# The first gate group of mixer B in seven block products, and pairs of heads 28 slots apart, in a hybrid convolution and attention layer

## The chip, the cores and the metric

The kernel runs on one core of one Trainium2 chip. The metric is the device time of one execution in microseconds; of several runs the median is taken. A lower time is better.

## What is computed

One decoder layer on 512 tokens of width 2048, in float32, with two mixers side by side:

```
h = rms_norm(x, norm_g)
a_val, a_glu, a_gate, q, k, v, b_gate = split(h @ w_in)     # seven blocks of 1024 columns

u = a_val * sigmoid(a_glu)                                  # mixer A
u = causal_depthwise_conv(u, conv_w, conv_b)                # 31 taps
u = silu(layer_norm(u, conv_norm_g, conv_norm_b))
y_a = (u @ conv_pw_w + conv_pw_b) * silu(a_gate)

q, k = rms_norm per head (16 heads of 64)                   # mixer B
o = dilated_attention_mixture(q, k, v)                      # (128,1), (512,4), (2048,16)
y_b = o * silu(b_gate)

out = x + concat(y_a, y_b) @ w_out
```

The three dilated patterns share one softmax: a table adds the logarithm of the number of patterns that see a key to its score, or a large negative number.

## The kernel before

**Precision.** All large products take float32 operands as two float16 halves: a high part and the low remainder. A product is three matmuls (high times high, high times low, low times high; `tri`, lines 414 to 416). The high halves are copies on ScalarE (ACT), the low halves scalar_tensor_tensor on VectorE (DVE, all through the wrapper at line 82). Scales that keep the halves in range come from sums of squares ("bounds": `measure` and `row_squares`, an ACT pass into `junk`, line 192).

**Groups and units.** The input product is cut into groups of 512 output columns, listed in `GROUPS` in the order in which TensorE (PE) takes them: `vg` 0 to 3 (value and GLU gate of mixer A), `q`, `k`, `v` and `bg` (gate of B) of each half of the heads, `ag` (gate of A); then `pw` 0 and 1 (the pointwise projection, which reads the split convolution result `u16`), `wb` and `wa` (output product). A group of the input product has four units of 512 rows of weights; `pw` has two. A unit of a plain group has eight slots of six 512-column matmuls each. `vg` 0 and 1 are computed in float32.

**Seven block products.** Groups in `SEVEN` take a two-by-two block scheme with seven products instead of eight (`input_products`). Sums of weight blocks are made by accumulating DMAs on POOL's queue and by two DVE subtractions; sums of activation blocks (`tx`) are made once. Each half of a block sum is split by itself (`hi` on ACT, `lo` on DVE, five and four slots ahead of its matmuls), the products land in four PSUM banks, and ACT copies (`copy`) and DVE joins (`joint`, `fourth`) put them together before `out` hands a quarter on. Such a group has 28 slots of twelve 256-column matmuls; the slot clock counts them as 32.

**Slots, calendar and planner.** All instructions are put out in an order written by hand. A clock counts slots, eight to a unit (unit 32 begins at slot 256, `pw` 0 at slot 448). `after(n, fn)` puts work n slots later. In every slot, what is due goes first, then `run_conv`, then the slot's matmuls. Each engine works its own instructions strictly in that order, so a wait holds up all that stands behind it on its engine.

**The convolution** is a generator (`conv`). Its 240 taps are DVE instructions on 512 columns, two channel blocks at a time. `run_conv` gives it DVE time: the wrapper charges every DVE instruction with `START` (180 ns) and 25/24 ns per element, each slot takes `PACE` off (1480 once pairs run), and taps go in while the balance is negative. A `yield n` in the generator waits n slots. After the last tap comes the layer norm: mean (matmul L576), differences and squares, variance (`token_rsqrt`, matmul L395), the row of reciprocal roots (matmul L408, copy L409), then per channel block a multiplication, a Silu (L609) and the split into `u16` (L316 and a DVE low half). Mean and variance are held back while a pair of heads is in its first eight slots:

```python
while any(0 <= clock[0] - n < 8 for n in at_pair.values()):
    yield 1
```

At the start of a unit of `pw`, splits that it needs and that are not yet put out are forced.

**Attention** works on pairs of heads (`two_heads`): scores (L741) on PE in slots 0 and 3 of a pair, the softmax's maxima on DVE, exponentials on ACT (L754), high and low halves of the probabilities (L765, `low`), a DMA transpose on SP's queue (`turn`), and the products with v (L782) at the pair's end, in the slot in which the next pair starts. `attention` puts eight pairs at every 32nd slot: 226, 258, 290, 322, 354, 386, 418, 450. The score buffers (`att` pool) hold the sums `tx` until the last group in seven products is done.

**Gates.** A gate group's results go through Silu into `slot` tiles; `gate_o` multiplies a pair's output with its gate and adds its squares to the bound of the output product. `b0_parts` splits the first half of B's output and is put out 10 slots ahead of `pw`.

**Buffers.** Raw weights have a ring of 8, split weights (`part`) 4 tiles, `slot` 35, `tmp` 4, `att` 4; PSUM has 4 banks for products and 4 for the rest. The split of unit i + 1 (`wh`, L301) is put out in the first slot of unit i and takes the tiles of unit i - 1.

Of the kernel before, what the change touches and what calls it, by code (L numbers as in the profile page):

```python
# [15 lines left out]
AF = mybir.ActivationFunctionType  # L16
# [16 lines left out]
H = S // 2  # L33
WARM = 9
KU = 4
PERIOD = {0: 32, 1: 32}
PHASE = 2
START = 180
NORM_FROM = 37
PACE = 1230  # L40
RMS_EPS = 1e-6
# [6 lines left out]

GROUPS = [("vg", 0), ("vg", 1), ("vg", 2), ("vg", 3), ("q", 0), ("k", 0), ("v", 0), ("bg", 0), ("q", 1), ("k", 1), ("v", 1),
          ("ag", 0), ("ag", 1), ("bg", 1), ("pw", 0), ("pw", 1)]  # L50
JOINED = (0, 1)
GROUPS += [("wb", g) for g in range(4) if g not in JOINED] + [("wa", g) for g in range(4)]
OUT_K = {"wb": (2,), "wa": (3, 0, 1)}

SEVEN = (("vg", 3), ("q", 0), ("v", 0))
LAST_SEVEN = SEVEN[-1]
# [30 lines left out]
def layer(ctx: ExitStack, tc: tile.TileContext, xt, w1, w2, w3, g_in, conv_w, conv_b,  # L87
# [34 lines left out]
    def after(n, fn):  # L122

        calendar.setdefault(clock[0] + max(n, 1), []).append(fn)
# [384 lines left out]
    def evac_qk(half_i, t, ps, is_k):  # L509
        r = evac_scale(("k" if is_k else "q", half_i))  # L510
        z = slot("z")
        sq = temp("sq")
        if is_k:
            V.scalar_tensor_tensor(by_head(z), by_head(ps), r, gp[:, None, :].to_broadcast([P, 8, DH]),
                                   op0=OP.mult, op1=OP.mult)
        else:
            A.activation(z, ps, AF.Copy, scale=r)
        A.activation(sq, ps, AF.Square, scale=r)
        n = [2, 6 + 4 * t, 7 + 4 * t, 9 + 4 * t]
        if is_k and ("v", half_i) in SEVEN:  # L520
# [24 lines left out]
    def conv():  # L545
# [24 lines left out]
        for i in (6, 7):  # L570
            V.tensor_add(acc, acc, cv[i])
        yield 3
        while any(0 <= clock[0] - n < 8 for n in at_pair.values()):
# [10 lines left out]
        for i in range(8):  # L584
            V.tensor_sub(cv[i], cv[i], mean_sb)
            if len(squares) > 1:
                V.tensor_add(acc2, acc2, squares.pop(0))
            if i == 0:
                A.activation(acc2, cv[i], AF.Square)
            else:  # L590
                squares.append(temp("lnsq"))
                A.activation(squares[-1], cv[i], AF.Square)
# [12 lines left out]
        for i in range(8 + 2):  # L605
            if i < 8:
                V.tensor_mul(cv[i], cv[i], row)
            if 1 <= i < 8 + 1:
                A.activation(cv[i - 1], cv[i - 1], AF.Silu, scale=lng[:, i - 1:i], bias=lnb[:, i - 1:i])  # L609
# [81 lines left out]
    def b0_parts():  # L691
        y = yf["b0"]
        s = scales["yb0"][0]
        for k in range(4):
            after(2 * k, lambda k=k: plain("b0", k, s))
        for k in range(2):
            after(6 + 3 * k, lambda k=k: y_sums("d", y, k, k + 2))
            for n, name in enumerate(("t34d", "t12d")):
                after(9 + 3 * k + n, lambda name=name, k=k: block(name, k, s))

# [16 lines left out]
    def two_heads(pair):  # L717
# [77 lines left out]
        plan = [(0, lambda: scores(((3,),))), (3, lambda: scores(((0, 2), (1,))))]  # L795
        for a, e in ((0, 7), (1, 11)):
            h = (13, 18)[a]
            plan += [(6, lambda a=a: shift(a)), (e + 4, lambda a=a: roots(a)), (h + 6, lambda a=a: turn(a))]
            for i in range(NT):
                plan += [(e, lambda a=a, i=i: exps(a, i))]  # L800
                plan += [(h + i // 2, lambda a=a, i=i: high(a, i)), (h + 3 + i // 2, lambda a=a, i=i: low(a, i))]
        return plan, values, put
# [8 lines left out]
    def attention(hf):  # L811
        start = max(clock[0] + 28, max(at_pair.values(), default=0) + PERIOD[0])
        start += (PHASE - start) % 8
        for p4 in range(4):
            at_pair[4 * hf + p4] = start + p4 * PERIOD[hf]

            def begin(pair=4 * hf + p4):
# [8 lines left out]
                after(PERIOD[hf] - (pair == 7), lambda: end_pair(pair))  # L826
            after(at_pair[4 * hf + p4] - clock[0], begin)
# [326 lines left out]
    def input_products(i0):  # L1154
# [82 lines left out]
        def out(name):  # L1237
# [6 lines left out]
            if kind == "vg":  # L1244
# [10 lines left out]

                after(1, mul)
            elif kind == "v":
                if n == 0:
# [5 lines left out]
            else:  # L1264
# [9 lines left out]

                norm_qk(group, t, sq, (2, 5, 6, 8), to)

# [72 lines left out]

    calendar.setdefault(8 * of_group["pw", 0][0] - 10, []).append(b0_parts)  # L1350
    for i in range(n_plain):
# [137 lines left out]
```

## Time and profile before

| | |
|---|---|
| median of 3 runs | 813.09 us (812.22 to 813.32) |
| profiled execution, time | 812.95 us |
| its span, first to last instruction | 811.2 us |
| granted TensorE clock | 1.000 |
| busy: PE, DVE, ACT, POOL | 805.5, 707.2, 561.3, 136.2 us |

The span lies within the execution's time; the 1.75 us between them are outside the instructions. In rows of instructions the first number is the start in microseconds from the span's start, the second the duration, then engine, line, operation, output and inputs; in square brackets is the engine's idle time just before, and what ended it. Matmul rows overlap: a 512-column matmul shows 0.38 us while the next one starts after 0.216.

### The profile page before, as it was taken

The numbers are of one execution on the slowest core, as the hardware profiler recorded it, in microseconds if no ns is written. First come the engines' busy times: TensorE is split into PE (matmuls) and PEld (weight loads), VectorE is DVE, ScalarE is ACT, GpSimd is POOL, SyncE is SP. The second block draws the span as 40 slices with busy tenths as digits, with TensorE's granted clock in tenths as the row PEclk, the third lists the DMA queues.
The fourth block names the chain that finished last, engine by engine and source line by source line (L and its number), as shares of the span: only waits on it lengthen the run. The fifth ranks groups of instructions, "written<-read, shape, count | busy, mean of one in ns | idle before, by whom it ended". The sixth has DMA issues, their size and how long they took to land.

```text
span 811.2 us, 13603 instructions
## 1 busy us (share of the span) xinstructions
PE 805.5 (99%) x5341; PEld 508.8 (63%) x5341; DVE 707.2 (87%) x1188; ACT 561.3 (69%) x788; POOL 136.2 (17%) x147
## 2 busy tenths in 40 slices
PE   9999999999999999999999999999999999999998
PEld 6888745888646854444444444444444447888887
DVE  6668999878989979999999989996689799979885
ACT  6667687577756688586756747587699968965541
POOL 0001021322223400004012010000100003432420
PEclk9999999999999999999999999999999999999999
DMA  9952345983875882526573634426352397898752
GB/s 337 355 212 91 117 93 144 136 255 57 308 150 108 121 296 94 128 104 169 143 182 102 164 112 125 118 88 165 104 120 102 110 278 165 170 249 198 131 103 68
DMA packets 100000, 127.19 MB, mean 157 GB/s; under 512 B 62560, under 2 KB 85344, under 8 KB 90720
## 3 DMA queue, kind: packets, MB, share of 16 engines
q1 hardware_dynamic: 80544, 107.37, 42.2%
q0 software_dynamic: 19104, 18.88, 16.3%
q8 instruction: 41, 0.67, 0.3%
q14 instruction: 23, 0.19, 0.1%
q10 hardware_dynamic: 288, 0.07, 0.0%
HBM read 88.56 MB, written 4.19 MB: 114 GB/s over the span
## 4 chain that ended last, share of the span: by engine, by line
PE 92%; DVE 4%; ACT 2%; DMA 1%; issue 1%; POOL 0%; ACTq 0%; DVEq 0%
PE ps_l L414 24%; PE ps_l L415 24%; PE ps_l L416 24%; PE ps_l L895 10%; PE ps_s L415 2%; PE ps_s L414 2%; PE ps_s L416 2%; PE ps_o L782 2%; PE ps_s L741 2%; DVE ws L82 1%; DMA pt<-hl 1%; DVE wl L82 1%; ACT junk L192 0%; DMA wf<-w_dram 0%; DVE cv L82 0%
## 5 line engine op out<-in xcount | busy, mean ns | idle before, releaser
L82 DVE SCALAR_TENSOR_TENSOR cv<-u,cw,cv 128x511 f32<-128x511 f32 (+14 forms) x240 | 162.0, 728 | 0.4 <-ACT cv L552 0.4
L192 ACT ACTIVATE junk<-wf 128x2048 uint8<-128x2048 f32 x68 | 129.2, 1900 | 9.4 <-DMA wf<-w_dram 9.0
L414 PE MATMUL ps_l<-x,wh 128*128 128x512 f16 x320 | 121.3, 379 | 0.4 <-DVE glu L82 0.4
L416 PE MATMUL ps_l<-x,wl 128*128 128x512 f16 x320 | 121.3, 379 | 0.0
L415 PE MATMUL ps_l<-x,wh 128*128 128x512 f16 x320 | 121.3, 379 | 0.0
L301 ACT ACTIVATE wh<-wf,ws 128x2048 f16<-128x2048 f32 x42 | 83.7, 1994 | 52.0 <-PE ps_l L415 50.2
L82 DVE SCALAR_TENSOR_TENSOR wl<-wf,ws,wh 128x2048 f16<-128x2048 f32 x43 | 100.9, 2346 | 12.1 <-ACT wh L301 12.1
L414 PE MATMUL ps_l<-wh,x 128*128 128x512 f16 x256 | 97.1, 379 | 0.0
L416 PE MATMUL ps_l<-wh,x 128*128 128x512 f16 x256 | 97.0, 379 | 0.0
L415 PE MATMUL ps_l<-wl,x 128*128 128x512 f16 x256 | 97.0, 379 | 0.0
L82 DVE SCALAR_TENSOR_TENSOR ws<-wf,ws 128x1024 f16<-128x1024 f32 x70 | 89.2, 1279 | 7.0 <-ACT ws L1173 4.5
L414 PEld LDWEIGHTS <-wh 128*128 128x128 f16 x448 | 43.9, 98 | 51.5 <-issue 4.0
L416 PEld LDWEIGHTS <-wl 128*128 128x128 f16 x448 | 43.8, 98 | 50.0 <-DVE wl L82 0.4
L415 PEld LDWEIGHTS <-wh 128*128 128x128 f16 x448 | 43.8, 98 | 47.1 <-issue 0.8
L895 PE MATMUL ps_l<-xr,wr 128*128 128x512 f32 x288 | 69.9, 398 | 0.1
L895 PEld LDWEIGHTS ps_l<-xr,wr 128*128 128x128 f32 x288 | 54.5, 190 | 13.7 <-ACT xr L339 1.0
L206 POOL TENSOR_SCALAR ws<-ws 128x1 f32<-128x1 f32 x20 | 9.4, 470 | 306.9 <-DVE ws L82 259.8
L414 PEld LDWEIGHTS <-x 128*128 128x128 f16 x352 | 34.4, 98 | 32.5 <-issue 1.9
L416 PEld LDWEIGHTS <-x 128*128 128x128 f16 x352 | 34.4, 98 | 31.3
L415 PEld LDWEIGHTS <-x 128*128 128x128 f16 x352 | 34.4, 98 | 30.1
L1173 ACT ACTIVATE ws<-wf,ws 128x1024 f16<-128x1024 f32 x42 | 47.1, 1138 | 5.7 <-PE ps_l L416 4.8
L170 POOL TENSOR_TENSOR ss<-ss,half 128x8 f32<-128x8 f32 x16 | 31.5, 1970 | 116.4 <-DVE ss L82 116.3
(265 smaller groups left out, 1871.3 us busy)
## 6 DMA issues: line engine op xcount, KB each, us to landing
wf<-w_dram SPq DMA_DIRECT2D x72, 1024.0 KB, 5.2
wf<-wf POOLq DMA_DIRECT2D x30, 512.0 KB, 6.3
x<-xt_dram SPq DMA_DIRECT2D x16, 256.0 KB, 6.6
res<-xt_dram SPq DMA_DIRECT2D x8, 512.0 KB, 6.7
out_dram<-res SPq DMA_DIRECT2D x15, 256.0 KB, 3.8
wf<-w_dram SPq DMA_DIRECT2D x7, 512.0 KB, 7.2
wf<-wf POOLq DMA_DIRECT2D x12, 256.0 KB, 5.8
wf<-w_dram SPq DMA_DIRECT2D x2, 256.0 KB, 3.4
```

The costliest lines, as they stand in the source:

```text
L82: return getattr(self.engine, name)(out, src, *args, **kw)
L170: G.tensor_tensor(ap, ap, half.to_broadcast(list(ap.shape)), op=OP.pow)
L192: A.activation(junk[:, :n], src, AF.Square, scale=scale, accum_out=acc)
L206: G.tensor_scalar(scale, scale, 1e-30, 2.0 ** (-2 * top), op0=OP.max, op1=OP.mult)
L301: A.activation(parts[i][0], raw[i], AF.Copy, scale=wscale[units[i][3:]][0])
L414: T.matmul(ps, ah, bh, start=first, stop=False, skip_group_check=more)
L415: T.matmul(ps, ah, bl, start=False, stop=False, skip_group_check=more)
L416: T.matmul(ps, al, bh, start=False, stop=last, skip_group_check=more)
L741: T.matmul(ps[i, a], qk["q", hf][p4 // 2][rows, p4 % 2, q, i * P:w], qk["k", hf][p4 // 2][rows, p4 % 2, k, :w], start=n == 0, stop=n == 2)
L782: T.matmul(po[rows, i * P:(i + 1) * P], vs[hf][j // 2][:, j % 2, 2 * p4 + a, vp * DH:(vp + 1) * DH], got["t", a][:, pp * (ALL // P) + FROM ...
L895: T.matmul(banks[group, m], wt[:, a, m * P:(m + 1) * P], xk[b], start=k == 0 and a == b == 0, stop=k == KC - 1 and a == 1)
L1173: A.activation(t[:, 0], block(name, pair), AF.Copy, scale=wscale[group][0])
```

## The change

- `bg` 0 goes in front of `v` 0 and into `SEVEN`. The order is now q, k, bg, v (slots 128 to 255). Its quarters go through Silu in `out`, eight halves of 256 columns; two tiles come together as one gate, and `gate_o` is called.
- `bg` 1 goes in front of `ag` 1: `bg` 1 has slots 384 to 415, `ag` 1 has 416 to 447.
- Pairs of heads stand every 28 slots, from slot 258 (60 slots behind the end of `k` 0): 258, 286, 314, 342, 370, 398, 426, 454. The steps within a pair are drawn together: exponentials at 7 and 10, high halves from 11 and 15, low halves two slots behind them, transposes at 16 and 20. The products of the last pair stay at slot 481.
- `PACE` goes from 1230 to 1300. The yields in the layer norm are shorter.
- `b0_parts` is put out 1 slot ahead of `pw` and in closer steps.
- Normalisation of q and k in `input_products` is put out two to four slots later; the copy `p5` of `bg` and `v` takes a `tmp` tile instead of a `slot` tile.

```diff
-PERIOD = {0: 32, 1: 32}
+PERIOD = 28
...
-PACE = 1230
+PACE = 1300
...
-GROUPS = [("vg", 0), ("vg", 1), ("vg", 2), ("vg", 3), ("q", 0), ("k", 0), ("v", 0), ("bg", 0), ("q", 1), ("k", 1), ("v", 1),
-          ("ag", 0), ("ag", 1), ("bg", 1), ("pw", 0), ("pw", 1)]
+GROUPS = [("vg", 0), ("vg", 1), ("vg", 2), ("vg", 3), ("q", 0), ("k", 0), ("bg", 0), ("v", 0), ("q", 1), ("k", 1), ("v", 1),
+          ("ag", 0), ("bg", 1), ("ag", 1), ("pw", 0), ("pw", 1)]
...
-SEVEN = (("vg", 3), ("q", 0), ("v", 0))
+SEVEN = (("vg", 3), ("q", 0), ("bg", 0), ("v", 0))
...
-        if is_k and ("v", half_i) in SEVEN:
+        if is_k and half_i == 0:
...
@@ conv
-        yield 3
+        yield 2
...
-            yield 1 + i % 2
+            yield 1
...
-        yield 4
+        yield 3
...
-            yield 1
+            yield (i + 1) % 2
             if i >= 2:
                 u16[i - 2] = split16(cv.pop(i - 2), scales["u"][0], "u16")
...
@@ b0_parts
-            after(2 * k, lambda k=k: plain("b0", k, s))
+            after(1 + k, lambda k=k: plain("b0", k, s))
...
-            after(6 + 3 * k, lambda k=k: y_sums("d", y, k, k + 2))
+            after(4 + 3 * k, lambda k=k: y_sums("d", y, k, k + 2))
...
@@ two_heads
-        for a, e in ((0, 7), (1, 11)):
-            h = (13, 18)[a]
-            plan += [(6, lambda a=a: shift(a)), (e + 4, lambda a=a: roots(a)), (h + 6, lambda a=a: turn(a))]
+        for a, e in ((0, 7), (1, 10)):
+            h = (11, 15)[a]
+            plan += [(6, lambda a=a: shift(a)), (e + 3, lambda a=a: roots(a)), (h + 5, lambda a=a: turn(a))]
...
@@ attention
-        start = max(clock[0] + 28, max(at_pair.values(), default=0) + PERIOD[0])
+        start = max(clock[0] + (28 if hf else 60), max(at_pair.values(), default=0) + PERIOD)
...
@@ input_products
-            got[to] = slot("cb")
+            got[to] = temp("cb") if to == "p5" and kind in ("bg", "v") else slot("cb")
...
+            elif kind == "bg":
+                for m in range(2):
+                    i = 4 * g + 2 * x + m
+                    if ("bg", i) not in u_part:
+                        u_part["bg", i] = slot("gate")
+                    A.activation(u_part["bg", i][:, z * H:(z + 1) * H], pair[:, m], AF.Silu)
+                    halves["bg", i] = halves.get(("bg", i), 0) + 1
+                    if halves["bg", i] == 2:
+                        bg[i] = u_part.pop(("bg", i))
+                        after(1, lambda i=i: gate_o(i))
...
-                norm_qk(group, t, sq, (2, 5, 6, 8), to)
+                norm_qk(group, t, sq, (2, 7, 8, 10) if n == 0 else (4, 9, 10, 12), to)
...
-    calendar.setdefault(8 * of_group["pw", 0][0] - 10, []).append(b0_parts)
+    calendar.setdefault(8 * of_group["pw", 0][0] - 1, []).append(b0_parts)
```

More of the change, by code (lines that the diff above doesn't have):

```diff
@@ L694, in b0_parts @@
         for k in range(4):
-            after(2 * k, lambda k=k: plain("b0", k, s))
+            after(1 + k, lambda k=k: plain("b0", k, s))
         for k in range(2):
-            after(6 + 3 * k, lambda k=k: y_sums("d", y, k, k + 2))
+            after(4 + 3 * k, lambda k=k: y_sums("d", y, k, k + 2))
             for n, name in enumerate(("t34d", "t12d")):
-                after(9 + 3 * k + n, lambda name=name, k=k: block(name, k, s))
+                after(6 + 3 * k + n, lambda name=name, k=k: block(name, k, s))
     def y_parts(s, v):
@@ L795, in two_heads @@
         plan = [(0, lambda: scores(((3,),))), (3, lambda: scores(((0, 2), (1,))))]
-        for a, e in ((0, 7), (1, 11)):
-            h = (13, 18)[a]
-            plan += [(6, lambda a=a: shift(a)), (e + 4, lambda a=a: roots(a)), (h + 6, lambda a=a: turn(a))]
+        for a, e in ((0, 7), (1, 10)):
+            h = (11, 15)[a]
+            plan += [(6, lambda a=a: shift(a)), (e + 3, lambda a=a: roots(a)), (h + 5, lambda a=a: turn(a))]
             for i in range(NT):
                 plan += [(e, lambda a=a, i=i: exps(a, i))]
-                plan += [(h + i // 2, lambda a=a, i=i: high(a, i)), (h + 3 + i // 2, lambda a=a, i=i: low(a, i))]
+                plan += [(h + i // 2, lambda a=a, i=i: high(a, i)), (h + 2 + i // 2, lambda a=a, i=i: low(a, i))]
         return plan, values, put
@@ L811, in attention @@
     def attention(hf):
-        start = max(clock[0] + 28, max(at_pair.values(), default=0) + PERIOD[0])
+        start = max(clock[0] + (28 if hf else 60), max(at_pair.values(), default=0) + PERIOD)
         start += (PHASE - start) % 8
         for p4 in range(4):
-            at_pair[4 * hf + p4] = start + p4 * PERIOD[hf]
+            at_pair[4 * hf + p4] = start + p4 * PERIOD
             def begin(pair=4 * hf + p4):
@@ L825, in begin @@
                         after(n, fn)
-                after(PERIOD[hf] - (pair == 7), lambda: end_pair(pair))
+                after(PERIOD - (pair == 7), lambda: end_pair(pair))
             after(at_pair[4 * hf + p4] - clock[0], begin)
```

## The prediction

> **What bounds the kernel now.** I began with the busy table and the chain of waits, then asked what PE waited for, then cut the span into stages.
>
> ```profile
> span 811.2 us, 13603 instructions
> PE 805.5 (99%) x5341; PEld 508.8 (63%) x5341; DVE 707.2 (87%) x1188; ACT 561.3 (69%) x788; POOL 136.2 (17%) x147
> ...
> PE 92%; DVE 4%; ACT 2%; DMA 1%; issue 1%; POOL 0%; ACTq 0%; DVEq 0%
> ...
> PE ps_l L414 <- DVE glu L82: 0.4, 1, 0.4
> ...
> PE ps_l L415 <- DVE ws L82: 0.2, 1, 0.2
> PE ps_o L782 <- DMA pt<-hl: 0.2, 1, 0.2
> PE ps_s L741 <- DVE gate L82: 0.2, 1, 0.2
> ```
>
> The last rows are three of the five waits that PE had after its start; the five, from 0.4 down to 0.2, are 1.3 us together. So the time is the number of matmuls times their pitch, and a change pays on PE or nowhere, unless it opens a wait. DVE is at 87%, which is no bound on the average, but it has deadlines.
>
> ```profile
> 212.58 0.38 PE L414 MATMUL ps_l<-wh,x 128*128 128x512 f16 x1
> ...
> 254.04 0.27 PE L414 MATMUL ps_l<-ws,x 128*128 128x256 f16 x1
> ...
> 290.75 0.38 PE L414 MATMUL ps_l<-x,wh 128*128 128x512 f16 x1
> ...
> 175.50:212.60 37.10, 36.88 (x340) 32.90 (x338) 31.91 (x40) 26.35 (x31) 9.33 (x8) 1.00 0.66 155
> 254.00:290.75 36.75, 36.75 (x338) 32.90 (x337) 33.34 (x43) 22.83 (x28) 14.60 (x11) 1.00 0.86 148
> ```
>
> The first three rows are the first matmuls of three groups in a row. k of the first half, plain, takes 254.04 - 212.58 = 41.46 us, 1.296 a slot. v of the first half, in seven products, takes 290.75 - 254.04 = 36.71. The last two rows give q0's and v0's stages (length, then PE, weight loads, DVE, ACT, POOL busy, clock, DMA share): q0, right behind another group of seven products, is 0.2 us short of a full PE.
>
> **The change, part by part.**
>
> *The first gate group of B in seven products* takes out 192 matmuls of 512 columns and puts in 336 of 256: 41.46 - 36.71 = 4.75 us less PE, all of it on the path. This is the one gain in PE work; pairs, orders and yields move matmuls and remove none.
>
> *What it adds to DVE.* Four plain splits become 14 half ones, two subtractions and four joins.
>
> ```profile
> L82 DVE SCALAR_TENSOR_TENSOR wl<-wf,ws,wh 128x2048 f16<-128x2048 f32 x43 | 100.9, 2346 | 12.1 <-ACT wh L301 12.1
> L82 DVE SCALAR_TENSOR_TENSOR ws<-wf,ws 128x1024 f16<-128x1024 f32 x70 | 89.2, 1279 | 7.0 <-ACT ws L1173 4.5
> ...
> 266.28 0.68 DVE L82 SCALAR_TENSOR_TENSOR cb<-ps_l,cb 128x512 f32<-128x512 f32 x1
> 266.88 1.22 DVE L82 TENSOR_TENSOR wf<-wf 128x1024 f32<-128x1024 f32 x1
> ```
>
> 14 x 1.28 + 2 x 1.22 + 4 x 0.68 - 4 x 2.35 = 13.7 us more, in a group 4.75 us shorter. What gives way is the convolution, which takes DVE time as the planner grants it. So no wait at this spot: v0 stood behind k0 before, with 33.34 us of DVE in 36.75, and did not stop PE; the gates need no DVE. The bound for two such groups back to back is q0: 0 to 0.4 us (37.10 against 36.71); I take 0. The six accumulating transfers on POOL's queue and the reloads that SP issues as blocks come free are those of v0's group, whose 0.86 DMA share also stopped nothing: 0. ACT has 22.83 us in 36.75 there; 14 half splits and eight half-width Silus fit.
>
> *q0's normalisation two slots later*, out of the way of POOL's power, removes at most q0's 0.2 us: -0.2.
>
> *PACE 1230 to 1300* lets the convolution take 5% more of each slot before the pairs.
>
> ```profile
> 536.92 3.22 DVE L82 SCALAR_TENSOR_TENSOR cv<-u,cw,cv 128x484 f32<-128x484 f32 x5
> ```
>
> Five taps in a row take 3.22 us, 0.64 each, where the planner charges 0.68 (180 + 484 x 25/24 ns). So 1300 of charges are about 1.23 us of DVE, under the slot's 1.296: 0, with 0 to 0.7 (one tap) as bounds.
>
> *Pairs every 28 slots from slot 258*, instead of every 32 from 226. The last pair's values stay at slot 481. Within a pair, low halves, transpose and values keep their distances (10 and 8 slots to the values).
>
> ```profile
> 326.37 1.28 DVE L82 SCALAR_TENSOR_TENSOR hl<-sx,st,hl 128x384 f16<-128x384 f32 x2
> ...
> pt<-hl SPq DMA_TRANSPOSE x16, 5.4
> ...
> 336.98 1.86 PE L782 MATMUL ps_o<-pt,v 128*64 128x128 f16 x60
> ```
>
> Pair 0: 327.65 plus 5.4 to land is 333.1, 3.9 us ahead of the values. Cover stays: 0, up to 1 if ACT's shorter exponential chain runs late.
>
> *The end of the convolution.* I added the planner's own charges (180 plus n x 25/24 per instruction, against PACE or 1480 a slot) up over the slots of both orders. For before this puts the last tap in slot 399; for after, slots 414 to 415: 91 taps are done by slot 256 instead of 97, and by 414 five whole pairs have been paid for.
>
> ```profile
> 540.06 1.41 DVE L82 TENSOR_TENSOR lnacc<-lnacc,cv 128x512 f32<-128x512 f32 x2
> 542.77 1.02 PE L576 MATMUL ps_s<-lnacc,ones 128*128 128x512 f32 x2
> 578.77 0.79 PE ps_s L395 x8
> 584.76 0.47 PE ps_s L408 x2
> 608.41 0.38 PE L414 MATMUL ps_l<-u,wh 128*128 128x512 f16 x1
> ```
>
> Before agrees: the sums of slot 399 start at 540.06, the mean stands in slot 402 at 542.77, the variance (L395) in slot 426, the row (L408) in 430, and pw's first matmul, slot 448, is 608.41. The mean had 1.3 us to spare; the shorter yield uses that up: 0, at most 1. For after the mean falls in slot 416 or 417 and the variance would be due in 432 or 433. But 426 to 433 are the first eight slots of pair 6, in which the layer norm holds back. So it goes in 434 and the row in 438: ten slots ahead of pw's first, where there were eighteen. The quicker yields put the split u16 at slots 444 to 454, the fourth forced out as pw begins.
>
> *What ACT must then do before pw's fourth operand.* PE is in order and needs it in its second slot.
>
> ```profile
> 559.83 0.68 ACT L468 ACTIVATE gate<-ps_l,esc 128x512 f32<-128x512 f32 x1
> 560.40 1.15 ACT L592 ACTIVATE lnsq<-cv 128x512 f32<-128x512 f32 x2
> ...
> 575.98 2.00 ACT L301 ACTIVATE wh<-wf,ws 128x2048 f16<-128x2048 f32 x1 [7.09 <-PE ps_l L415]
> 578.00 1.28 ACT L754 ACT_TABLE_LOAD   x1
> ...
> 586.78 1.90 ACT L765 ACTIVATE hl<-sx,st 128x128 f16<-128x128 f32 x4
> 588.59 1.99 ACT L301 ACTIVATE wh<-wf,ws 128x2048 f16<-128x2048 f32 x1
> 590.59 1.28 ACT L609 ACT_TABLE_LOAD   x1
> 591.89 0.81 ACT L609 ACTIVATE cv<-cv,lnb,lng 128x512 f32<-128x512 f32 x1
> 592.61 1.90 ACT L192 ACTIVATE junk<-wf 128x2048 uint8<-128x2048 f32 x1
> ...
> 594.50 0.79 ACT L765 ACTIVATE hl<-sx,st 128x128 f16<-128x128 f32 x2
> ...
> 598.94 0.70 ACT L316 ACTIVATE u<-cv,us 128x512 f16<-128x512 f32 x1
> 599.55 0.71 ACT L688 ACTIVATE y<-gate,yb0s 128x512 f16<-128x512 f32 x1
> ...
> 608.18 0.71 ACT L316 ACTIVATE u<-cv,us 128x512 f16<-128x512 f32 x1
> 609.03 0.74 DVE L82 SCALAR_TENSOR_TENSOR u<-cv,us,u 128x512 f16<-128x512 f32 x1
> ```
>
> wh at 575.98 is slot 424's: it waited for PE to free the buffer, so it cannot run early. From it to the next wh, 588.59, are 12.61 us: split, table load, eight exponentials with one bound (junk), row copy, four high halves. After has just these from slot 432 to 440. Then come, start to start: split 2.00, four highs 1.81, table load 1.30, four gates at 0.57, five Silus at 0.72, a bound 1.89, four splits at 0.61: 15.32. With the low half on DVE, 0.74: 12.61 + 15.32 + 0.74 = 28.67 us after slot 432 begins. PE wants it after 16 slots (20.73), variance and row (0.79 + 0.47), and 2.17 into pw (a slot, half of one, a matmul): 24.16. PE waits 28.67 - 24.16 = **4.5 us**. The same rule for before: wanted at 608.41 + 2.17 = 610.58, ready at 609.77, 0.8 spare, and PE shows no wait there. Moving b0_parts behind slot 448 and the two gate products out is in the sum (their four splits aren't in it). One slot earlier or later moves it by 1.3: 3.2 to 5.8. The four splits for the second half of pw's first group come some 3 us in time once PE has waited (ACT's next 11 us are three Silus, four splits, a wh, a bound and five y parts; PE has six slots and pair 7 ahead of them): 0.
>
> The two table loads follow the instruction ahead of them at once: 577.98 to 578.00. The Trainium skill, "ScalarE: Activation LUTs", section "What ACT_TABLE_LOAD costs", adds a drain of about 1.38 us to each load. By that the wait would be, as an estimate, 2.8 us longer; these rows show no drain beside the load, so I leave it out.
>
> *Sum.* The profiled execution took 812.95 (span 811.2), 0.14 under the median 813.09. 812.95 - 4.75 - 0.2 + 4.5 = 812.5; beside the median, **812.6**.
>
> **Rivals.**
>
> *The gain comes through.* The variance goes ahead of pair 6, by slot 425. The row is then nine slots earlier, ACT has 11 us more and the wait is gone: 812.6 - 4.5 = 808.1. For it: before has eighteen slots there, and no wait. Against it: taps would have to end by 407, and I count 414.
>
> *A later layer norm.* If the taps end past slot 416, nothing holds the variance any longer and every slot costs 1.3 us of PE. Two microseconds of charges more (three taps) put their end at 420 by the same count, the variance at 438, and the price at 4 x 1.3 = 5.2: 817.8. For it: one to two slots of margin. Against: the count met before exactly.
>
> *PE at half rate after its wait.*
>
> ```profile
> 0.98 4.02 PE L148 MATMUL ps_s<-wz 128*128 128x512 f16 x9 [0.98 <-POOL wz L145]
> ```
>
> Nine warming matmuls take 4.02 us, 0.45 each, twice the 0.216 (1.296 / 6) later. Should the wait bring this back for as long, it costs 2.0: 814.6. Against: the wait is in pieces, a matmul or two at each split that arrives. The Trainium skill, "TensorE: Matmul & The Clock Gate", Part 1, has the clock halve after an idle window of about 3.4 us; it speaks against this change if the wait is in one piece. The clock is 1.00 in all stages quoted, so no row of before tests it.
>
> *The drain on table loads*, by bounds from the rows, would make ACT two gaps longer; no row shows one. It gets 0.02, within the last case below.
>
> **How the numbers follow.** My forecast has 0.60, own range 810.9 to 814.6 (wait 3.2 to 5.8, up to 0.7 for denser DVE). A measurement tells about 0.2% from no change: 811.5 to 814.7. Of the 0.60, 0.13 lies under 811.5. The gain in full has 0.20, the later layer norm 0.12, half rate and the other additions, at the upper edge and counted as slower, 0.08. That makes faster 0.33, same 0.47, slower 0.20. The range holds the full gain and the half rate and leaves out the later layer norm: 807.8 to 815.6.
>
> **What would show it.** The gate group between k0 and v0 lasts 36.7 us (37.1 if back to back costs). pw's first matmul comes at 608.41 - 4.95 = 603.5. The variance matmul (L395, eight) is near 584.1, later than 578.77 in spite of the gain. PE has 4 to 5 us of waits at 603 to 610, on DVE's u (L82) behind ACT's u (L316), and the chain of waits runs through ACT there. If the variance stands near 574 and PE doesn't wait, the first rival is right; if it stands past 588, the second. Waits of PE on ws in the gate group or v0 would make the part on DVE wrong; on pt, the part on pairs. A clock under 1.00 behind pw's start is the third.

## The result, and the profile after

The changed kernel takes 839.53 us (838.76 to 840.85) against 813.09: a ratio of 1.033, interval 1.031 to 1.035. It is slower by 26.4 us, where 0.5 us of gain was forecast. The profiled execution took 840.85, 27.9 more than that of before.

The page of the changed kernel: span, busy table, chain of waits.

```profile
span 839.0 us, 13948 instructions
...
PE 810.9 (97%) x5485; PEld 524.2 (62%) x5485; DVE 719.6 (86%) x1204; ACT 572.9 (68%) x807; POOL 147.3 (18%) x154
...
PE 53%; DVE 26%; ACT 13%; issue 4%; DMA 3%; POOL 1%; SPq 0%; ACTq 0%; DVEq 0%
```

PE's share of the chain falls from 92% to 53%, DVE's rises from 4% to 26%, with DVE's busy share a point lower: DVE is late, not fuller. What PE waits for (total, times, longest):

```profile
PE ps_s L204 <- DVE st L82: 5.8, 3, 3.6
PE ps_l L416 <- DVE wl L82: 3.3, 3, 1.8
PE ps_l L415 <- DVE ws L82: 3.2, 3, 1.3
PE ps_l L414 <- DVE glu L82: 2.5, 1, 2.5
PE ps_l L415 <- DVE u L82: 2.2, 5, 0.5
PE ps_l L414 <- ACT wh L301: 1.9, 1, 1.9
PE ps_l L414 <- ACT u L316: 1.7, 3, 0.7
PE ps_o L782 <- DMA pt<-hl: 1.7, 1, 1.7
```

These eight kinds are 22.3 us; before, all waits behind the start were 1.3. They are on nearly every kind of operand: `st` holds the row maxima that DVE takes out of the score banks, `pt` the transposed probabilities, `wh` and `wl` the two halves of a unit of weights, `ws` those of a block sum, `u` the splits of `u16`, `glu` the gate of mixer A.

The same execution in stages (length, then PE, weight loads, DVE, ACT, POOL busy; granted clock, DMA share, GB/s): `vg` 2; gate group; v0; slots 258 to 426 (pairs 0 to 5); 17 us within them; slots 426 to 448; the first six slots of `pw`, with pair 6's values; from pair 7's start to its values.

```profile
99.38:142.39 43.01, 43.01 (x194) 19.15 (x193) 40.25 (x69) 29.24 (x37) 5.54 (x6) 0.96 0.46 124
257.98:294.75 36.77, 36.77 (x339) 32.82 (x338) 34.99 (x45) 25.32 (x33) 18.40 (x16) 1.00 0.93 123
294.75:336.03 41.28, 37.34 (x340) 32.87 (x337) 33.51 (x41) 26.99 (x30) 5.41 (x7) 1.00 0.84 249
338.90:592.45 253.55, 245.63 (x1526) 114.48 (x1525) 230.06 (x440) 181.37 (x279) 30.33 (x32) 0.99 0.47 130
542.80:560.00 17.20, 13.54 (x117) 6.38 (x117) 16.39 (x36) 6.47 (x8) 2.98 (x3) 0.80 0.24 71
592.45:625.10 32.65, 31.93 (x171) 14.95 (x168) 20.65 (x52) 25.61 (x43) 4.14 (x5) 1.00 0.44 128
625.10:638.49 13.39, 10.72 (x97) 5.10 (x97) 10.44 (x14) 13.39 (x19) 0.00 (x0) 1.00 0.13 24
638.49:684.59 46.10, 40.59 (x191) 16.98 (x187) 38.06 (x81) 31.66 (x56) 1.23 (x5) 0.93 0.41 122
```

One row of before is needed beside them, a stage of 32 slots with one pair:

```profile
338.78:384.09 45.31, 45.31 (x281) 21.25 (x278) 44.16 (x83) 33.19 (x50) 8.68 (x8) 1.00 0.44 123
```

A pair adds 45.31 - 32 x 1.296 = 3.8 us of PE, so six stages of 28 slots need 6 x 40.1 = 240.8, with the mean's matmuls 0.9 more: 241.7. They took 253.55. DVE was busy for 97% of before's stage and stopped nothing; here it is 91% and PE waits. The ledger of the 27.9 us:

| stretch | against before | forecast |
|---|---|---|
| up to `vg` 2 (99.38 for 97.20) | +2.2 | 0 |
| `vg` 2 (43.01 for 41.59) | +1.4 | 0 |
| `vg` 3 and q0; k0 | -0.4; +0.7 | -0.2; 0 |
| gate group of B (36.77 for 41.46) | **-4.7** | -4.75 |
| v0 (41.28 for 36.71) | +4.6 | 0 |
| slots 258 to 426 (253.55 for 241.7) | **+11.8** | 0 |
| first six slots of `pw` | **+4.6** | +4.5 |
| what is left, nearly all behind them | +7.7 | 0 |

Two of these sizes vary from execution to execution. Up to slot 256 four runs below put out the same instructions as the changed kernel (shifted sums, pairs 24 and 32 apart, PACE_2 1400, early variance); the gate group and v0 together took 76.7 to 82.1 us in them, 78.05 here. The +1.4 of `vg` 2 came in only one of the four.

The +4.6 of `pw` is read from these rows: the last matmul ahead of it, the variance, the first and last that wait, and the last of the six slots.

```profile
604.79 0.95 PE L395 MATMUL ps_s<-ones,lnacc 128*128 128x2 f32 x8
...
624.00 0.38 PE L416 MATMUL ps_l<-x,wl 128*128 128x512 f16 x1
625.10 0.38 PE L414 MATMUL ps_l<-u,wh 128*128 128x512 f16 x1 [0.72 <-ACT u L316]
...
630.99 0.38 PE L415 MATMUL ps_l<-u,wh 128*128 128x512 f16 x1 [0.41 <-DVE u L82]
...
636.38 0.38 PE L416 MATMUL ps_l<-u,wl 128*128 128x512 f16 x1
```

From 624.00 to 636.38 are 12.4 us for 36 matmuls of 0.216 (7.8): 4.6 too many. PE waits seven times, 0.41 to 0.72 us, 3.4 together; each wait costs 0.16 more than its gap, since a row shows 0.38 for a pitch of 0.216. The clock stays at 1.00.

### The profile page after: what moved, and what is told of

Read it like the earlier page. It is cut to its first block, busy times and chain, and to the rows that moved or that the text cites. A ratio compares the mean times of both kernels' runs of the same rounds, so it can differ in the third digit from the quotient of the medians.

```text
span 839.0 us, 13948 instructions
## 1 busy us (share of the span) xinstructions
PE 810.9 (97%) x5485; PEld 524.2 (62%) x5485; DVE 719.6 (86%) x1204; ACT 572.9 (68%) x807; POOL 147.3 (18%) x154
## 4 chain that ended last, share of the span: by engine, by line
PE 53%; DVE 26%; ACT 13%; issue 4%; DMA 3%; POOL 1%; SPq 0%; ACTq 0%; DVEq 0%
PE ps_l L414 12%; PE ps_l L415 12%; PE ps_l L416 12%; PE ps_l L895 9%; DVE cv L82 8%; DVE wl L82 5%; ACT sx L754 4%; ACT junk L192 3%; DVE ws L82 2%; DVE hl L82 2%; PE ps_s L416 2%; PE ps_s L414 2%; PE ps_s L415 2%; DVE sx L82 2%; ACT wh L301 2%
## 5 line engine op out<-in xcount | busy, mean ns | idle before, releaser
L82 DVE SCALAR_TENSOR_TENSOR ws<-wf,ws 128x1024 f16<-128x1024 f32 x84 | 107.0, 1278 | 12.1 <-ACT ws L1173 9.6
L82 DVE SCALAR_TENSOR_TENSOR wl<-wf,ws,wh 128x2048 f16<-128x2048 f32 x39 | 91.5, 2347 | 14.1 <-ACT wh L301 14.1
L414 PE MATMUL ps_l<-x,wh 128*128 128x512 f16 x256 | 98.8, 386 | 2.5 <-DVE glu L82 2.5
L416 PE MATMUL ps_l<-x,wl 128*128 128x512 f16 x256 | 98.5, 385 | 0.4 <-DVE wl L82 0.4
L415 PE MATMUL ps_l<-x,wh 128*128 128x512 f16 x256 | 98.6, 385 | 0.0
L301 ACT ACTIVATE wh<-wf,ws 128x2048 f16<-128x2048 f32 x38 | 75.7, 1993 | 28.2 <-PE ps_l L415 27.2
L416 PEld LDWEIGHTS <-wl 128*128 128x128 f16 x384 | 38.1, 99 | 51.1 <-issue 6.6
L414 PEld LDWEIGHTS <-wh 128*128 128x128 f16 x384 | 38.2, 99 | 50.5 <-issue 9.5
L1173 ACT ACTIVATE ws<-wf,ws 128x1024 f16<-128x1024 f32 x56 | 62.8, 1139 | 9.3 <-PE ps_l L416 7.9
L415 PEld LDWEIGHTS <-wh 128*128 128x128 f16 x384 | 38.1, 99 | 46.2 <-issue 8.9
L206 POOL TENSOR_SCALAR ws<-ws 128x1 f32<-128x1 f32 x20 | 10.4, 518 | 280.6 <-DVE ws L82 280.2
```

The costliest lines, as they stand in the source:

```text
L82: return getattr(self.engine, name)(out, src, *args, **kw)
L206: G.tensor_scalar(scale, scale, 1e-30, 2.0 ** (-2 * top), op0=OP.max, op1=OP.mult)
L301: A.activation(parts[i][0], raw[i], AF.Copy, scale=wscale[units[i][3:]][0])
L414: T.matmul(ps, ah, bh, start=first, stop=False, skip_group_check=more)
L415: T.matmul(ps, ah, bl, start=False, stop=False, skip_group_check=more)
L416: T.matmul(ps, al, bh, start=False, stop=last, skip_group_check=more)
```

## Where the pairs lose time

The largest single wait, on PE and then on DVE:

```profile
549.66 1.43 PE L741 MATMUL ps_s<-qk,qk 64*128 64x128 f16 x18
554.68 0.16 PE L204 MATMUL ps_s<-wsum,ones 128*128 128x2 bf16 x1 [3.60 <-DVE st L82]
554.71 0.59 PE L414 MATMUL ps_l<-x,wh 128*128 128x512 f16 x1
555.09 0.63 PE L415 MATMUL ps_l<-x,wh 128*128 128x512 f16 x1
...
559.78 0.46 PE L414 MATMUL ps_l<-x,wh 128*128 128x512 f16 x1
```

```profile
550.47 3.26 DVE L82 SCALAR_TENSOR_TENSOR cv<-u,cw,cv 128x488 f32<-128x488 f32 x5
553.65 0.28 DVE L82 CUSTOM_DVE_ANT_0 sx<-ps_s,tab 128x128 f32<-128x128 f32 x1
```

A sum of bounds (slot 401, a two-column matmul) stands right behind the second scores of a pair and needs a score bank that DVE has not read yet, because the planner has put five taps, 3.26 us, ahead of the reading. Behind it the product's matmuls come every 0.43 us for 5 us: half rate. The small matmul costs 3.6 us and then 12 x 0.21 = 2.5 more. In the changed kernel pairs begin at slots 286 and 398, three ahead of the sums of slots 289 and 401; in before the nearest begin at 290 and 386, one behind the first and fifteen ahead of the second.

In the whole stretch of slots 258 to 426 PE is idle for 7.9 us (253.55 - 245.63), and the half rate adds 2.5: 10.4 of the 11.8.

## The experiments

Ratios are against before on the same chip. Edits are of the changed kernel except where before is named.

**Which part costs it: the pairs alone, in before.** PERIOD, the steps and the start of the pairs are those of the changed kernel; nothing else is.

```diff
-PERIOD = {0: 32, 1: 32}
+PERIOD = 28
-        start = max(clock[0] + 28, max(at_pair.values(), default=0) + PERIOD[0])
+        start = max(clock[0] + (28 if hf else 60), max(at_pair.values(), default=0) + PERIOD)
...  (and the new steps of two_heads)
```

> The kernel before with the pairs of the changed kernel alone: every 28 slots from slot 258, their steps drawn together; gate group plain and behind v, PACE 1230, old order of gate groups, old yields. By the planner's charges the taps end in slot 406 and the variance is held back to slot 434, as in the changed kernel. Theory A (pairs that stand off the beat of eight slots and the layer norm behind pair 6 carry most of the loss by themselves): 830 to 840 us, PE waits on st at the bound sums of slots 289 and 401, stages of pairs 1, 5 and 6 some 1.5 to 7 us over their ideal, a wait of 4 to 5 us at pw's start. Rival B (the pairs cost only because the seven products and PACE 1300 had made DVE late): 815 to 822 us, pair stages within 1 us of their ideal, the wait at pw's start alone (4 to 5 us) and what follows it.

835.18 us, 1.029 (1.027 to 1.031): +22.8 of the 26.4. Slots 258 to 426, then `pw`'s first slots with pair 6's values, and what PE waited for between 600 and 650 us:

```profile
334.44:588.03 253.59, 246.85 (x1523) 115.89 (x1523) 223.12 (x427) 172.47 (x268) 29.47 (x31) 0.98 0.48 127
...
625.88:643.00 17.12, 13.92 (x96) 5.89 (x96) 13.49 (x20) 15.23 (x21) 0.00 (x0) 0.67 0.24 73
```

```profile
PE ps_l L414 <- ACT u L316: 6.6, 2, 5.9
PE ps_l L415 <- DVE u L82: 2.5, 2, 2.3
```

The pairs' stretch is as long as in the changed kernel, 253.6, with the gate group plain and PACE at 1230. Theory A held in the time and in the waits on st; at `pw`'s start PE waited 9.1 us, where it had 4 to 5. The layer norm slips too: the last tap goes from slot 399 to 406 by the planner's charges, the variance from 426 to 434. Here the waits at `pw` come in larger pieces (the longest 5.9 and 2.3 us), and the clock falls to 0.67 over the 17.12 us.

**The steps alone, in before** (exponentials at 7 and 10 and so on, pairs still 32 apart from slot 226).

> The kernel before with one part of the change alone: the steps within a pair drawn together (exponentials at 7 and 10, high halves from 11 and 15, transposes at 16 and 20), pairs still 32 slots apart from slot 226, taps ending in slot 399 and variance in slot 426 as before. Theory A (distance: it is the pair's work every 28 slots that leaves the in-order engines no slack): 812 to 814 us. Rival B (the steps drawn together, which leave 3 slots in place of 4 between an exponential and what reads it, are what makes the pairs wait): 818 to 826 us, with waits on st and pt in the stages of the pairs.

813.15 us, 1.0004 (0.9994 to 1.0014). The closer steps cost nothing that shows. What is left of the edit is the place of the pairs: the distance of 28 slots and the start in slot 258, which no run parts.

**The late layer norm alone, in before.**

```diff
-        yield 4
+        yield 15
```

> The kernel before with one number changed: 15 in place of 4 slots to wait ahead of the variance, which so stands in slot 434 (426 before) and the eight splits in slots 445 to 455 (437 to 451 before), as in the kernel before with the changed pairs alone. Pairs stay 32 apart. Theory A (the late layer norm by itself stops PE at pw's start and brings half rate behind the wait, some 15 us there with the changed pairs): 822 to 828 us. Rival B (the lateness costs only what the path from variance to pw's fourth operand lacks, some 4 to 5 us as in the changed kernel, and the rest came from the pairs): 815 to 819 us.

822.30 us, 1.012 (1.010 to 1.014): +9.7.

```profile
611.25 0.38 PE L414 MATMUL ps_l<-u,wh 128*128 128x512 f16 x1 [2.06 <-ACT u L316]
...
616.63 0.58 PE L415 MATMUL ps_l<-u,wh 128*128 128x512 f16 x1 [2.30 <-DVE u L82]
```

```profile
608.98:621.00 12.02, 6.54 (x31) 2.31 (x31) 10.08 (x19) 11.57 (x17) 0.00 (x0) 0.63 0.14 59
```

5.5 us of waits at `pw`'s start (0.41 and 0.70 lie between the two rows), and most of the rest is half rate (clock 0.63 over 12 us). So the pairs' 22.8 are, as an estimate from two runs, about 9.7 through the layer norm and about 12 in their own stretch (253.6 - 241.7).

**Pairs 24 and 32 slots apart in turn**, all on the beat of eight slots on which units and bound sums stand, in the changed kernel and in before with the pairs alone.

```diff
-            at_pair[4 * hf + p4] = start + p4 * PERIOD
+            at_pair[4 * hf + p4] = start + p4 * PERIOD - 4 * (p4 % 2)
...
-                end_pair(pair - 1)
...
-                after(PERIOD - (pair == 7), lambda: end_pair(pair))
+                after(PERIOD + 3 * (pair == 7), lambda: end_pair(pair))
```

> The changed kernel with pairs 24 and 32 slots apart in turn (258, 282, 314, 338, 370, 394, 426, 450) in place of 28 throughout: the same mean distance and the same work, but every pair starts on the beat of eight slots on which units and bound sums stand. The values come 28 slots behind a pair's start, those of the last at slot 481 as before; variance in slot 434 and splits as in the changed kernel. Theory A (the loss in the pairs is their place against the eight-slot beat): the waits on st at slots 289 and 401 go, the stretch of slots 258 to 426 is some 8 to 12 us shorter, 827 to 832 us. Rival B (the pairs are too dense for the in-order engines at seven eighths of the distance, wherever they stand): 836 to 843 us, the waits at other places.

> The same turn of 24 and 32 slots in the kernel before with the pairs of the changed kernel alone (835.2 us with 28 throughout). Theory A (beat): 822 to 828 us, the stretch of slots 258 to 426 within 3 us of its ideal (it has 14 over it with 28), the wait at pw's start staying. Rival B (density): 832 to 838 us.

848.05 us, 1.044 (1.041 to 1.047), and 838.12 us, 1.032 (1.030 to 1.033). The waits on st at slots 289 and 401 went, and others came: scores (L741) waited 4.1 us and values (L782) 8.7 and 3.3 us for DVE's st. Slots 258 to 426 took 259.6 and 254.2 us, no less than with 28 throughout (253.6). I had held the beat for the cause, and theory A predicted 8 to 12 us less. But the values stand behind the next pair's scores in this edit, so that the beat by itself is neither shown nor ruled out; the runs say only that this order doesn't mend it.

**The bound sums of slots 289 and 401 six slots later.**

```diff
-                after(4, lambda: bound("w", ...
+                after(4 + 6 * (clock[0] in (283, 395)), lambda: bound("w", ...
```

> The changed kernel with two of the sums of a bound (one small matmul each) put out 6 slots later, in slots 295 and 407. With pairs every 28 slots, the pairs of slots 286 and 398 begin four slots off the beat of the units, and these sums fell in their slot 3, right behind the second scores; the matmul takes a score bank that DVE has yet to read, and PE waited 1.9 us at 387 and 3.6 us at 555, with some 2.6 us at half the granted clock behind the second. Theory A: both waits and the slow matmuls go, 7 to 8 us less: 832. Theory B: DVE's delay meets PE at the next split (wl) instead; 2 us or less are won: 837.5 to 839.5.

839.64 us, 1.033. The bound sums' waits on st fell from 5.8 to 0.3 us, but the mean now waited 2.2 us for lnacc, the sums of the layer norm, and the stretch was only 1.7 us shorter (251.85). The time of the whole is unchanged. (The profiled execution also waits 3.2 us for ACT's ws, in v0; that lies ahead of the edit.)

**The taps' share lowered:** PACE_2 = 1400.

> The changed kernel with PACE_2, the time that a slot is granted once pairs run, at 1400 in place of 1480, so that the taps leave DVE more room among the pairs; by the planner's charges they end in slot 423 in place of 408 and the variance stands in slot 447, which must cost at pw's start some 15 us more. Read by stages. Theory A (DVE is granted more than its slots hold among the pairs): slots 258 to 426 last 243 to 247 us in place of 253.6, no wait on st over 1 us. Rival B (not the taps' share but the order of pair, weights and bounds makes the waits): 250 to 256 us there.

843.90 us, 1.038 (1.036 to 1.040). Slots 258 to 426 took 248.3 us, 5.2 less, between both theories. Of the 5.2, 0.9 is the mean's matmuls, which stand in slot 434 here, behind this stretch; so fewer taps took 4.3 of the 11.8 away. The price fell due at the layer norm: variance and row are forced out as `pw` begins, with waits of 4.2 and 3.4 us. Slots 426 to 454 took 57.9 us for 46.0, some 11 more without the mean, where I had reckoned 15.

**Relief of one engine or both.** Taps on half of the columns; bounds over a quarter of the weights; both. Order and charges stay.

> The changed kernel, every tap of the convolution done on 256 of its 512 columns (the other half is left out); the planner charges it as before, so that the order of all instructions is the same. Five taps in a row took 3.22 us; half ones should save about 0.3 us each, 70 us of DVE in all. Theory C (DVE has more work than time from the float32 start to the projection): the waits on glu, wl, the score banks and lnacc go, the waits at the start of pw (ACT, in order) stay: 813 to 820. Theory D (ACT is the engine without slack, DVE's lateness follows from it): over 830.

> The changed kernel, the bound of every unit of weights taken over 512 of its 2048 columns (three quarters of the squares are left out); same order of all instructions. A bound takes 1.90 us on ACT and should take about 0.6, some 1.3 us less, 68 times: about 85 us of ACT. Theory C: the waits on DVE stay as they are; at pw two shorter bounds stand ahead of the fourth split, 2 to 3 us, and v 0 keeps its wait for the loads: 832 to 837. Theory D: PE's waits shrink all over: 813 to 822.

> The changed kernel with both reliefs at once: taps on 256 of 512 columns (leaves out half of the convolution) and bounds of the weights over 512 of 2048 columns, charged and ordered as before. Either alone took some 15 us off. Theory A (one chain through both in-order engines, relieved already by either): 816 to 822 us, and what stays are waits that are a matter of order: pw's first operands (variance in slot 434) and the sums that wait for a score bank. Rival B (two separate shortages that add up): 808 to 812 us, as 839.5 - 15 - 15 = 809.5, with under 2 us of waits after the start.

825.16 us, 1.016 (1.014 to 1.017); 824.64 us, 1.015 (1.013 to 1.016); both 818.79 us, 1.008 (1.006 to 1.009). Either engine's relief takes 14 to 15 us off, both 20.7, not 29: the two do not add, as would be so if one chain ran through DVE and ACT in many places and shortening either link opened it; the runs do not follow that chain. With both it is still 6 us over before. What stays in its profile is mostly waits for wl and wh within `pw` (4.2 us), for `pw`'s first operands u (1.8) and for st (1.5).

**PACE 1300 alone, in before.**

> The kernel before with PACE 1300 and no other edit. The planner puts the first tap in slot 55 instead of 88 and ends the taps in 385 instead of 399. If the start of the changed kernel is rightly read, vg 2 begins 1.5 to 2.5 us late and works 0 to 1.5 us longer; later DVE is ahead of its old schedule and no other wait appears: 815 to 817. If the higher pace alone makes DVE late all over, more: 820 to 830.

825.10 us, 1.015 (1.013 to 1.017): +12.7, where I had said 0 to 0.7. Its stage up to `vg` 2 is 2.0 longer, `vg` 2 1.6, and pair 6's stage 8.5. There the layer norm comes *earlier*, among pair 6's exponentials:

```profile
584.65 1.28 ACT L754 ACT_TABLE_LOAD   x1
...
588.60 1.28 ACT L609 ACT_TABLE_LOAD   x1
...
594.55 1.28 ACT L754 ACT_TABLE_LOAD   x1
...
598.52 1.28 ACT L609 ACT_TABLE_LOAD   x1
```

```profile
610.62 0.61 PE L416 MATMUL ps_l<-x,wl 128*128 128x512 f16 x1 [4.32 <-DVE wl L82]
```

Two stretches of Silus and splits stand ahead of the next unit's wh, four table loads between them, and PE waits for wl, which follows wh.

**The variance ahead of pair 6, in the changed kernel** (a yield shorter by one, so that it goes in slot 425).

> The changed kernel with the last yield ahead of the variance at 2 instead of 3. The planner's count has the taps end in slot 408 and the variance due in 426, the first slot in which pair 6 holds it back until 434. One slot less puts it in 425 and the splits of u16 nine slots earlier. Theory A: the waits of PE on u at the start of pw (4.6 us over the stretch) go, and part of the 8 us that the rest of pw is too long, since ACT is no longer behind: 827 to 835, most likely 831. Theory B: ACT and DVE are full in this stretch, the earlier splits push wh, exponentials and pair 6 back, and PE waits for those: within 2 us of 839.5.

848.28 us, 1.044 (1.042 to 1.046), 8.8 over the changed kernel: the same collision, with four table loads between 609 and 624 us and a wait of 6.1 us for ACT at `pw`'s start. This was my rival "the gain comes through"; it would have been the worse case.

**The start, v0 and all mends.** PACE 1230 up to slot 64; the bounds measured 8 slots later behind bg; these two with the shifted sums.

```diff
-        pace = ... else PACE
+        pace = ... else PACE if clock[0] >= 64 else 1230
...
-                    after(MEASURE + (0, -1, 2, 3)[j], ...
+                    after(MEASURE + (0, -1, 2, 3)[j] + 8 * (kind == "bg"), ...
```

> The changed kernel with PACE at 1230 in the 64 slots of the float32 start, 1300 after it. Its profile shows the first taps put out in slot 55; two ACT copies and two taps stand ahead of the low halves and of glu, PE waits 2.5 us at 97 to 99 and then works about 1.4 us longer on vg 2 (43.0 instead of 41.6) at a lower granted clock. Theory A (separate waits, each with its own place): vg 2 begins near 97.2 and takes 41.6, and 3.6 us go: 836. The variance stays in slot 434, so nothing is given back there. Theory B (DVE has too much to do, and a wait that is taken away comes back at the next deadline): the taps that don't run at the start run later, the waits among the pairs grow, and the time stays within 1 us of 839.5.

> The changed kernel with the bounds (squares on ACT) of the weights that are loaded as the gate group of B frees its blocks put out 8 slots later. Theory A: in the stage of v 0 (41.25 us against 36.75) ACT stands 3.0 and 1.7 us in such a bound, waiting for a load of weights that SP issued late, behind transposes of k; its half splits come late and PE waits. Put out later, the bounds find the weights there: v 0 takes 36.7 to 37.5, and 4 us go: 835.5. Theory B: ACT's wait is only a symptom, DVE is behind anyway, and v 0 stays over 40 us: 838 to 840.

> The changed kernel with three mends at once: PACE 1230 up to slot 64, bounds of bg 0's follower measured eight slots later, the bound sums of slots 289 and 401 six slots later. Taps then end in slot 414 by the planner's charges, the variance stays in slot 434. Singly they gave +1, -3 and 0 us. Theory A (the waits are separate and mended together none finds another's place): 828 to 832 us: start and vg2 -3.4, v0 -3.3, pairs -3.5. Rival B (DVE and ACT are full from slot 256 on and a wait taken away comes back behind the next in-order step): 834 to 838 us.

840.65 us (1.035), 836.71 us (1.030), 836.14 us (1.031, 1.028 to 1.033). The first brought the start back (`vg` 2 begins at 97.45 and lasts 41.59) and lost it again to the later taps: slots 258 to 426 took 258.2 us, 4.6 more, 2.1 of it a wait of the mean for lnacc. The second took 3.3 us out of the gate group and v0 (78.05 to 74.80) and kept 2.8 of them. All three together stop at 836: stretch by stage the start is mended, the gate group with v0 nearly (74.5, where two groups of 36.7 are 73.4), the pairs are as long as ever (253.8), the mean alone waiting 4.6 us for lnacc.

**The gate group plain**, in its new place.

> The changed kernel with the first gate group of B plain, all else kept (its place in front of v, pairs every 28 slots, PACE 1300). By the forecast's count DVE has 13.7 us less to do and PE 4.75 us more; the planner then ends the taps in slot 390 and the variance goes in 408. Theory C: the waits after the start get small, pw's waits on u go; the start's 2.5 + 1.4 us stay, and the waits of two sums behind the second scores: 816 to 824. Rival E (pairs every 28 slots and the tight end are what hurts, not the seven products): over 830.

845.68 us, 1.041 (1.039 to 1.042), 6.1 over the changed kernel. These 6.1 are not what the seven products earn. Behind a plain gate group v0 takes 36.71 us and loses nothing; both together take 78.17, where the changed kernel takes 78.05. So at this spot v0 gives the 4.7 us of PE back. The 6.1 come later. The layer norm stands earlier, PE waits 8.8 us for DVE's diag and 6.6 for lnacc, two of its operands, and slots 258 to 426 take 270.0 us, 16.5 more; what follows is 11.3 shorter, without a wait on u at `pw`.

## Why the prediction was wrong

*Right, by its own steps.* The gate group lasts 36.77 (forecast 36.7). The variance goes in slot 434, held back by pair 6. PE loses 4.6 us at `pw`'s start (forecast 4.5), on ACT's u and DVE's. Those were the two large terms of my sum, and they cancel as I said.

There is luck in the second. The taps end in slot 408, not 414; the variance was then due in 426, the first slot in which pair 6 holds it, and one slot earlier it went through (the run with the early variance). That the clock stayed at 1.00 behind these waits is this execution's as well (last section). And of the signs that I had set, several spoke against me: the variance starts at 604.79, past my 588, though in the slot that I gave it; PE waited 3.2 us for DVE's ws in v0 and 1.69 us for pt at the values of pair 2; and the clock is 0.93 behind `pw`'s first slots.

*The step that failed* is "Cover stays: 0, up to 1" for the pairs every 28 slots: 11.8 in slots 258 to 426, and 12 in before with the pairs alone. I had priced the last step of a pair, its transpose against its values, and that step did run late once (1.69 us); I had not priced the first: DVE reads the scores between taps, and whatever PE has next in a score bank waits (5.8 us). With 32 slots before's DVE was busy 97% of a stage without one wait; that fit belonged to one order. What is shown: the place of the pairs costs it (the steps alone cost 0.4, by their interval at most 1.1), fewer taps take off 4.3, and relieving either in-order engine shortens the stretch (244.8 and 247.5 us with half taps and with quarter bounds, against 253.55). Which instructions would have to move for the rest stays open, and so does what distance and start each cost.

*The sum ended too early.* "The four splits for the second half of `pw`'s first group come some 3 us in time" nearly held: one wait on u follows, of 0.54 us.

```profile
646.33 0.38 PE L415 MATMUL ps_l<-u,wh 128*128 128x512 f16 x1 [0.54 <-DVE u L82]
```

But I priced nothing behind them, and most of the ledger's 7.7 us was lost there: 1.11, 1.91 and 1.78 us of waits for wl, wh and wl, and some 3 us by a clock of 0.93 over 46.10 us. The first row is the start of pair 7's eight exponentials on ACT, the second the wh of `pw`'s last unit behind them; then PE:

```profile
659.88 0.49 ACT L754 ACTIVATE sx<-sx,st,sc 128x128 f32<-128x128 f32 x1
...
666.22 1.99 ACT L301 ACTIVATE wh<-wf,ws 128x2048 f16<-128x2048 f32 x1
```

```profile
668.26 0.39 PE L414 MATMUL ps_l<-u,wh 128*128 128x512 f16 x1 [1.91 <-ACT wh L301]
...
670.65 0.61 PE L416 MATMUL ps_l<-u,wl 128*128 128x512 f16 x1 [1.78 <-DVE wl L82]
```

The half rate that I had as a rival at `pw`'s start, with 2.0 us, came here, and behind other waits.

*"PACE 1230 to 1300 ... 0, with 0 to 0.7"* failed. I added up how much DVE time a slot holds, not where the first taps go: from slot 55 instead of 88, in front of the GLU of `vg` 1, for which `vg` 2 waits. The two ACT copies that open them hold ACT's `wr` and with it DVE (2.32 us idle at 85.27, where before had 0.91 at 83.80); then come the taps, of which the first is shown.

```profile
87.40 0.73 DVE L82 SCALAR_TENSOR_TENSOR cv<-u,cw,cv 128x511 f32<-128x511 f32 x1
...
98.64 0.68 DVE L82 TENSOR_TENSOR glu<-ps_l,rrow 128x512 f32<-128x512 f32 x1
```

```profile
99.38 0.58 PE L414 MATMUL ps_l<-x,wh 128*128 128x512 f16 x1 [2.50 <-DVE glu L82]
99.76 0.63 PE L415 MATMUL ps_l<-x,wh 128*128 128x512 f16 x1
```

That is 2.2 us and, at half rate behind it, 1.4. It is also why my count of the taps' end was off: with 1230 up to slot 64 the mean stands in slot 417, as I had said, and not in 410. It changed nothing at the variance, since pair 6 held it anyway.

*The reloads on SP's queue, "0"*, were 4.6 in v0. The blocks that the gate group frees are loaded behind k's transposes; ACT's bounds wait for them, and the half splits behind those:

```profile
267.60 21.89 SPq L474 DMA_TRANSPOSE qk<-qhl  x6
289.66 0.45 SPq L267 DMA_DIRECT2D wf<-w_dram  x1
```

and on ACT:

```profile
296.75 1.91 ACT L192 ACTIVATE junk<-wf 128x2048 uint8<-128x2048 f32 x1 [3.02 <-DMA wf<-w_dram]
```

The 21.89 us hold 6.75 in which the queue itself waits for DVE. Before had the same order on the queue, but its first reload was issued 26.5 us behind the start of the group after k, here 31.7, and a plain group followed. I had reasoned from v0's DMA share behind a plain group (0.86, no wait). That ACT's bounds stand in front of the half splits is shown by the run that puts them later; that the order on the queue made the loads late is read from the rows and not tested.

## What to carry to other kernels

In an order written by hand, with engines that work strictly in order, "there is time in the slot" is no price for moving work: ask of each small instruction on the critical engine what it needs, and what the planner may put ahead of that on the other engine. A kernel whose PE waits nowhere while DVE is busy for 97% is tuned to its order: here the layer norm costs 9.7 us if it comes eight slots later and about as much (8.5 and 8.8) if it comes so early that it meets a pair's exponentials. A change that moves many things at once is best taken apart in the kernel before: the pairs alone told 22.8 of 26.4 us. But such prices don't add. PACE alone cost 12.7, which makes 35.5 for the two. The gate group alone, in before, was not run.

## What the chip showed

Half rate came behind waits much shorter than I had reckoned with, and not each time. A wait of 3.60 us was followed by 5 us of matmuls at 0.43 instead of 0.216 (rows above). With quarter bounds the same matmul waited 3.59 us, and the next ones came at the full rate:

```profile
542.95 0.16 PE L204 MATMUL ps_s<-wsum,ones 128*128 128x2 bf16 x1 [3.59 <-DVE st L82]
542.98 0.38 PE L414 MATMUL ps_l<-x,wh 128*128 128x512 f16 x1
```

`vg` 2 began behind a wait of 2.50 or 2.51 us in eight executions. Four showed half rate behind it, four did not; the row of the changed kernel stands above, this is the one with pairs 24 and 32 apart:

```profile
98.89 0.38 PE L414 MATMUL ps_l<-x,wh 128*128 128x512 f16 x1 [2.51 <-DVE glu L82]
99.10 0.38 PE L415 MATMUL ps_l<-x,wh 128*128 128x512 f16 x1
```

Even the seven short waits at `pw`'s start, 0.41 to 0.72 us within 6 us, were followed by eight matmuls at half rate in three of seven executions (1230 up to slot 64, bounds later, all mends), and by none in four, the changed kernel among them.

The Trainium skill, "TensorE: Matmul & The Clock Gate", Part 1, has an activity window of about 3.4 us that runs free of the program. The traces fit it in that the same wait went both ways; no run here shows where a window began. So in these runs a single wait of 2.5 to 3.6 us carried a second price of anything from nothing to 2.5 us, which no sum of waits shows.
